# Score matmuls of differential attention heads issued for one head or for two at a time, with PSUM in three pools or in one

## The chip, the cores and the metric

The kernel runs on one core of a Trainium2 chip. The time is that of one execution on the device, in microseconds (us). The engines are TensorE (PE; its weight loads, which overlap its matmuls, are listed as PEld), VectorE (DVE), ScalarE (ACT), GpSimd (POOL) and SyncE (SP). Each works through its own stream of instructions in order; semaphores tie the streams together. PSUM, where matmuls put their results, has eight banks.

## What is computed

Two layers of an encoder with 256 tokens and a width of 2048, all in f32. The part that the change touches is differential attention: eight heads, two softmax maps each, over keys of 64 features.

```python
def diff_attention(q, k, v, lam):
    b, s = q.shape[:2]
    qh = q.reshape(b, s, DIFF_HEADS, 2, DIFF_HEAD_DIM)
    kh = k.reshape(b, s, DIFF_HEADS, 2, DIFF_HEAD_DIM)
    scale = DIFF_HEAD_DIM ** -0.5
    ...
        scores = jnp.einsum('bqhcd,bkhcd->bhcqk', qb, kh).astype(jnp.float32) * scale
        probs = jax.nn.softmax(scores, axis=-1)
        weights = probs[:, :, 0] - lam * probs[:, :, 1]
        return jnp.einsum('bhqk,bkhe->bqhe', weights.astype(v.dtype), v)
```

Around it, in each layer: one wide projection of the normalised input (queries, keys and values of this attention, the latents of a second one, two gates), multi-head latent attention with eight heads (MLA), the two outputs weighed by the gates and projected, a SwiGLU feed-forward part, and a gated addition of a projected side input. A final norm ends it.

## The kernel before

**Products.** Nearly all the time goes into products of a weight matrix and activations. Activations lie with features on the partitions, 128 features by 256 tokens to a tile, 16 tiles for the width. To keep precision, each f32 operand is split into two parts of a faster format: a high part, and the remainder. A tile of activations (`ua`, `ub`) holds both, high in its left half and the remainder in its right. A *chunk* of a product (`emit`, L226 and L230) is two matmuls: the high weights against both halves (512 columns), and the weights' remainder against the high half (256 columns). A product of the full width has 16 chunks. Weights come by DMA, up to eight chunks to a piece (`piece`), into one of four buffers; ACT makes the high part `whi` (L201) and DVE the remainder `wlo` (L78), each in three buffers. `joined` adds the two halves of a finished PSUM bank: ACT copies one half to SBUF, DVE adds the other.

**The stage around the change.** `values` makes the values of the differential heads. `queries_keys(h)` makes the query and the key of head h, two full products, with a partial rotation and a split on DVE and ACT; heads 0 and 1 are made first. `scores` (L428) then multiplies query by key, with 64 features (half of the array's rows) for each of the two maps. A map is three products of parts (`three`), for two blocks of 128 queries: six matmuls, twelve for a head. The maps lie on the lower and the upper 64 partitions, and the matmuls alternate between them. `exps` takes the maximum of every row on DVE (L434) and the exponentials on ACT (L437). `diff_weights(h)` joins both maps to one matrix of weights, ACT and DVE sharing that work. `diff_out` first transposes the weights on TensorE (`turned`, L446), and in a second part multiplies them with the values (L701).

**Order.** A scheduler orders each engine's stream when the program is built, by the order in which instructions are traced and by when its own model of time has them ready; `keep_in_program_order` pins an instruction behind the one traced before it on its engine, `issue_after` behind a named one. `beside` is a generator of other work to fill in, in 16 steps: queries and keys of heads 2 to 7, the MLA keys (`keys_up`), its rotary key (`narrow`, `rotated`), then gate products, MLA queries (`queries_up`) and the norm of finished heads (`settle`). `pipelined` traces, for each head: one fill step, the weights of the *next* head, the transposes of this one, one fill step, the output of this one. The MLA heads go through the same `pipelined` with `mla_weights`, which also uses `scores`, and gate products as fill.

**PSUM.** Three pools share the eight banks: `ps_mm`, four, for products; `ps_s`, two, for scores; `ps_at`, two, for transposes, outputs and norms. The end of the kernel, where the last two products are cut into halves and the result is transposed and stored, takes banks of all three.

Of the kernel before, what the change touches and what calls it, by code (L numbers as in the profile page):

```python
# [12 lines left out]
F32 = mybir.dt.float32  # L13
# [3 lines left out]
ALU = mybir.AluOpType  # L17
AX = mybir.AxisListType

P = 128  # L20
# [36 lines left out]
def encoder(ctx, tc, x, p, positions, cols, lams, wq, wk, wv, wcq, wckv, wkr, wga, wgb,  # L57
# [6 lines left out]
    wts = pool("wts")  # L64
    tmp = pool("tmp")
    stat = pool("stat")
    ps_mm = pool("ps_mm", 4, space=PSUM)
    ps_s = pool("ps_s", 2, space=PSUM)
    ps_at = pool("ps_at", 2, space=PSUM)

    def scratch(tag, bufs, n=T):
        return tmp.tile([P, n], F32, tag=tag, name=tag, bufs=bufs)

    def bank(ps=ps_at, tag="at", name="at", shape=(P, 2 * T)):
        return ps.tile(list(shape), F32, tag=tag, name=name)

    def tt(o, a, b, op):
        return V.tensor_tensor(out=o, in0=a, in1=b, op=op)  # L78
# [155 lines left out]
    def product(src, us, inside=None):  # L234


        acc = bank(ps_mm, "mm", "mm")
        n = len(us)
        for a in range(0, n, PT):
            m = min(PT, n - a)  # L240
            hi, lo = piece(src[:, a * P : (a + m) * P], m)
            emit(acc, hi, lo, 0, us[a : a + m], a == 0, a + m == n, inside and (inside[0] - a, inside[1]))
        return acc

    def pair(src, us):

        n = len(us)
        hi, lo = piece(src.rearrange("n p m -> p n m"), 2 * n)
        for j in range(2):
            acc = bank(ps_mm, "mm", "mm")  # L250
            emit(acc, hi, lo, j * n, us, True, True)
            yield acc

# [146 lines left out]
    def narrow(src, us):  # L400


        acc = bank(ps_mm, "mm", "mm")
        w = wts.tile([P, PT * P], F32, tag="w32", name="w32", bufs=W_BUFS)
        nc.sync.dma_start(w, src)
        w = w.rearrange("p (c m) -> p c m", m=64)
        for a in range(0, NC, PT):
            both = wts.tile([P, PT * P + 64], F32R, tag="whi", name="whi", bufs=3)[:, : PT * P]
            hi, lo = (both.rearrange("p (c f m) -> p c f m", f=2, m=64)[:, :, f, :] for f in range(2))
            part = w[:, a : a + PT, :]  # L410
            A.activation(hi, part, AF.Copy)
            tt(lo, part, hi.bitcast(F32), ALU.subtract)
            for j in range(PT):
                PE.matmul(acc, both[:, j * P : (j + 1) * P], us[a + j], start=a + j == 0, stop=a + j == NC - 1)  # L414
        return acc
# [1 line left out]
    def three(q, k):  # L417
        return [(q[:, :T], k[:, T:]), (q[:, T:], k[:, :T]), (q[:, :T], k[:, :T])]

    def scores(*maps):  # L420


        Ss = [bank(ps_s, "S", "S", (P, 2, T)) for _ in maps]
        for b in range(2):
            for j in range(len(maps[0])):
                for S, pairs in reversed(list(zip(Ss, maps))):
                    q, k = pairs[j]
                    PE.matmul(S[:, b, :], q[:, b * P : (b + 1) * P], k, start=j == 0, stop=j == len(pairs) - 1)  # L428
        return Ss

    def exps(S, E, scale):

        nm, sm, rs = (stat.tile([P, 2], F32, tag=t, name=t, bufs=4) for t in ("nm", "sm", "rsum"))
        V.tensor_reduce(out=nm, in_=S, axis=AX.X, op=ALU.max, negate=True)  # L434
        ts(nm, nm, scale, None, ALU.mult)
        for b in range(2):
            last_exp[0] = A.activation(E[:, b, :], S[:, b, :], AF.Exp, bias=nm[:, b : b + 1], scale=scale, accum_out=sm[:, b : b + 1])  # L437
        V.reciprocal(out=rs, in_=sm)
        return rs
# [20 lines left out]
    def weights(tag="E", dt=F32):  # L460
        return tmp.tile([P, 2, T], dt, tag=tag, name=tag, bufs=2)
# [12 lines left out]
    def values(src, us, load=None):  # L474

        vals = stat.tile([P, 2, 2, 512], F32, tag="vals", name="vals", bufs=1)
        n = len(us)
        order = [(half, a, 2) for half in range(2) for a in range(0, n, 2)]
        if load:
            order = [(None, a, 1) for a in range(BOTH)] + [(half, BOTH, n - BOTH) for half in range(2)]  # L480
        banks = {}
        for half, a, m in order:
            if a == 0:
                for k in (0, 1) if half is None else (half,):
                    banks[k] = [bank(ps_mm, "mm", "mmv") for _ in range(2)]
            if load and not half:
                load(a, m)
            if half is None:
                hi, lo = piece([src[k][:, a * 512 : (a + 1) * 512] for k in range(2)], 8, 32, 16)
            else:  # L490
                hi, lo = piece(src[half][:, a * 512 : (a + m) * 512], 4 * m, 32, 16)
            for j in range(2 if half is None else m):
                k, c = (j, a) if half is None else (half, a + j)
                s = slice(j * 512, (j + 1) * 512)
                if load and c == 0:
                    first_chunk(banks[k], us[0], hi[:, s], lo[:, s])
                    continue
                for b in range(2):
                    xh = us[c][:, b * P : (b + 1) * P]
                    xl = us[c][:, T + b * P : T + (b + 1) * P]  # L500
                    PE.matmul(banks[k][b], xh, hi[:, s], start=c == 0, stop=False)  # L501
                    PE.matmul(banks[k][b], xl, hi[:, s], start=False, stop=False)  # L502
                    last_mm[:] = [PE.matmul(banks[k][b], xh, lo[:, s], start=False, stop=c == n - 1)]  # L503
            if half or a + m < n:
                yield
            if a + m == n:
                for b in range(2):
                    A.activation(vals[:, b, half, :], banks[half][b], AF.Copy)
                if not half:
                    yield vals  # L510
# [16 lines left out]
    for L in range(DEPTH):  # L527
# [153 lines left out]
        od, ods = [], ub[:8]  # L681
        ssd = stat.tile([P, 2 * DH], F32, tag="ssd", name="ssd", bufs=1)

        def diff_weights(h):
            q, k = qk[h]
            E = [weights(), weights("E1")]
            halves = [slice(c * 64, (c + 1) * 64) for c in range(2)]
            r = [exps(S, e, 0.125) for S, e in zip(scores(*(three(q[d], k[d]) for d in halves)), E)]
            ts(r[1], r[1], neg_lam[:, L : L + 1], None, ALU.mult)
            for b in range(2):  # L690
                A.activation(E[0][:, b, :], E[0][:, b, :], AF.Copy, scale=r[0][:, b : b + 1])
                stt(E[0][:, b, :], E[1][:, b, :], r[1][:, b : b + 1], E[0][:, b, :], ALU.mult, ALU.add)
            return E[0]

        def diff_out(h, W):
            wt = turned(W)
# [30 lines left out]
                next(out, None)  # L727
                W = nxt

        pipelined(diff_weights, diff_out, DH, lambda: next(fill, None))  # L730
        for _ in fill:
            pass
        vm, = (v for v in values(w_v[L], ckv) if v is not None)
# [3 lines left out]
        def mla_weights(h):  # L737
            E = weights()
            t = slice(h % 2 * T, (h % 2 + 1) * T)
            S, = scores(three(qn[h], kn[h]) + [(qr[h // 2][:, t], krs[1][:, t]), (qr[h // 2][:, t], krs[0][:, :T])])  # L740
            r = exps(S, E, MLA_SCALE)
            for b in range(2):
                ts(E[:, b, :], E[:, b, :], r[:, b : b + 1], None, ALU.mult)
            return E
# [104 lines left out]

    for n in ends:  # L850
        parts[n] = [piece(w_pg[L, n][:, a * P : (a + PT) * P], PT) for a in (0, PT)]
        m = banks[n, 0] = bank(ps_mm, "mm", "mm")
        for j, u in enumerate(ub):
            w, (hi, lo) = slice(j % PT * P, (j % PT + 1) * P), parts[n][j // PT]
            if j < whole[n]:
                matmul(m, hi[:, w], u, start=j == 0, stop=False)
            else:
                matmul(halves_of(m)[:, :, :P], hi[:, w], halves_of(u)[:, :, :P], start=False, stop=False)
            matmul(m[:, T:], lo[:, w], u[:, :T], start=False, stop=j == NC - 1)
    for n in ends:  # L860
        m = banks[n, 1] = bank(ps_mm, "mm", "mm")
        for j in range(whole[n], NC):
            w = slice(j % PT * P, (j % PT + 1) * P)
            matmul(halves_of(m[:, :T]), parts[n][j // PT][0][:, w], halves_of(ub[j])[:, :, P:], start=j == whole[n], stop=j == NC - 1)
        tiles_[n] = [scratch(tag, bufs) for tag, bufs in (("join", 3), ("a", 4), ("sig", 2))]
# [55 lines left out]
    def store(b, q, o):  # L921
        tc.keep_in_program_order(nc.sync.dma_start(out[b, :, q * 2 * T : (q + 2) * 2 * T], o))

    def S_bank():
        return operand(bank(ps_s, "S", "S", (P, 2, T)))

    def mm_bank():
        return bank(ps_mm, "mm", "mm")

    def steps(which, n):  # L930
        for _ in range(n):
            tc.keep_in_program_order(next(which))
# [6 lines left out]
    column = factors(0)  # L939
    for which, n in ((column, 2), (third, 1), (second, 2), (third, 2), (column, 2)):  # L940
        steps(which, n)
    t0 = [transposed(0, q, get()) for q, get in enumerate((S_bank, S_bank, mm_bank, mm_bank))]
    t1 = [transposed(1, 0, mm_bank())]
    column = factors(1)
    t1.append(transposed(1, 1, mm_bank()))
    t1.append(transposed(1, 2, bank()))
    parts_ = [rows() for _ in range(4)]
    left, right = slice(0, 2 * T), slice(2 * T, 4 * T)
# [3 lines left out]
    for j in range(2):  # L952
        tc.keep_in_program_order(scaled(parts_[j][:, right], t0[2 * j + 1], cols_[0], V))
        steps(column, 2)
        store(0, 2 * j, parts_[j])
    t1.append(transposed(1, 3, S_bank()))
    for j in range(2):
        tc.keep_in_program_order(scaled(parts_[2 + j][:, left], t1[2 * j], cols_[1], V))
        scaled(parts_[2 + j][:, right], t1[2 * j + 1], cols_[1], A)
# [89 lines left out]
```

## Time and profile before

| | |
|---|---|
| median of three runs | 2825.36 us (2825.22 to 2825.99) |
| the profiled execution | 2825.16 us |
| its span, first to last instruction | 2823.4 us |
| granted TensorE clock | 0.999 |
| DMA, mean over the span | 188 GB/s |

The profile is of one execution. Busy time of an engine is the union of its instructions. Matmuls are pipelined and overlap, so what a matmul costs TensorE is the distance from its start to the start of the next. The chain of waits follows the work that ended last back to its beginning. A row of the timeline has the start and the length in us, the engine, the line, the operation, what it writes and reads, and a count where like instructions in sequence are merged; in square brackets stands the idle time before it and what ended it. A group of a tile's or a line's instructions has the shortest, median and longest duration in ns, and the first and last start in us.

### The profile page before, as it was taken

How to read it: one execution, taken by the hardware profiler on the slowest of the kernel's cores; microseconds unless marked ns; L12 is line 12 of the kernel's file. 1: busy time of each engine (PE TensorE's matmuls, PEld its weight loads, DVE VectorE, ACT ScalarE, POOL GpSimd, SP SyncE). 2: the span in 40 equal slices, each digit the busy share in tenths (PEclk: the TensorE clock that was granted, in tenths of full speed). 3: DMA queues.
4: the chain of work that ended last, by engine and by line, in shares of the span. 5: the costliest groups of instructions: out<-in, count | busy, mean ns of one | idle time of the engine just before them, and what ended most of it. 6: DMA issues, size and time to landing. Idle time of an engine off the chain costs nothing.

```text
span 2823.4 us, 43989 instructions
## 1 busy us (share of the span) xinstructions
PE 2815.7 (100%) x16691; PEld 2490.2 (88%) x16691; DVE 2078.9 (74%) x3566; ACT 1531.1 (54%) x2554; POOL 3.1 (0%) x17
## 2 busy tenths in 40 slices
PE   9999999999999999999999999999999999999999
PEld 8888988888888888888888889888888888888888
DVE  8898668776666666677869976687766666666777
ACT  7676546554444444455646765465544444444556
POOL 0000000000000000000000000000000000000000
PEclk9999999999999999999999999999999999999999
DMA  7544455555665565565554454555556655655664
GB/s 247 175 161 172 157 186 198 194 193 194 187 200 193 188 194 198 194 193 193 194 193 166 157 172 158 194 198 194 193 194 189 199 194 184 203 193 194 193 193 157
DMA packets 158181, 531.36 MB, mean 188 GB/s; under 512 B 17169, under 2 KB 25361, under 8 KB 157969
## 3 DMA queue, kind: packets, MB, share of 16 engines
q1 hardware_dynamic: 157536, 527.96, 57.0%
q8 instruction: 131, 2.15, 0.3%
q10 hardware_dynamic: 432, 0.59, 0.1%
q14 instruction: 82, 0.66, 0.1%
HBM read 526.39 MB, written 2.10 MB: 187 GB/s over the span
## 4 chain that ended last, share of the span: by engine, by line
PE 100%; DMA 0%; DVE 0%; DVEq 0%; ACT 0%; SPq 0%; issue 0%
PE mm L226 61%; PE mm L230 31%; PE S L428 1%; PE mmv L502 1%; PE mmv L503 1%; PE mmv L501 1%; PE at L446 1%; PE at L701 1%; PE mm L848 0%; PE at L757 0%; PE mm L414 0%; PE at L716 0%; PE mmv L472 0%; DMA w<-in_wv 0%; PE at L339 0%; PE at L307 0%
## 5 line engine op out<-in xcount | busy, mean ns | idle before, releaser
L201 ACT ACTIVATE whi<-w 128x1024 fp32r<-128x1024 f32 (+2 forms) x1038 | 1064.3, 1026 | 1226.8 <-issue 593.3
L78 DVE TENSOR_TENSOR wlo<-w,whi 128x1024 fp32r<-128x1024 f32 (+2 forms) x1038 | 1224.9, 1181 | 647.8 <-ACT whi L201 638.7
L226 PE MATMUL mm<-ub,whi 128*128 128x512 f32 x3936 | 1340.5, 389 | 0.0
L226 PE MATMUL mm<-ua,whi 128*128 128x512 f32 x3712 | 1274.2, 390 | 0.0
L230 PE MATMUL mm<-ub,wlo 128*128 128x256 f32 x3936 | 1084.6, 276 | 0.0
L230 PE MATMUL mm<-ua,wlo 128*128 128x256 f32 x3712 | 1027.7, 277 | 0.0
L226 PEld LDWEIGHTS mm<-ub,whi 128*128 128x128 f32 x3936 | 737.8, 188 | 151.5
L226 PEld LDWEIGHTS mm<-ua,whi 128*128 128x128 f32 x3712 | 696.3, 188 | 141.2
L230 PEld LDWEIGHTS mm<-ub,wlo 128*128 128x128 f32 x3936 | 738.9, 188 | 1.3
L230 PEld LDWEIGHTS mm<-ua,wlo 128*128 128x128 f32 x3712 | 697.0, 188 | 2.0
L78 DVE TENSOR_TENSOR a<-mm,join 128x256 f32<-128x256 f32 (+1 forms) x423 | 174.5, 416 | 1.7 <-ACT join L877 1.4
L256 ACT ACTIVATE join<-mm 128x256 f32<-128x256 f32 x452 | 165.2, 367 | 6.4 <-PE mm L230 5.7
L78 DVE TENSOR_TENSOR xT<-xT,mm 128x256 f32<-128x256 f32 x256 | 106.8, 420 | 41.6 <-PE mm L230 37.7
L78 DVE TENSOR_TENSOR a<-a,row 128x256 f32<-128x256 f32 (+1 forms) x209 | 87.5, 422 | 5.9
L78 DVE TENSOR_TENSOR a<-a 128x256 f32<-128x256 f32 x120 | 50.9, 425 | 4.0
L78 DVE TENSOR_TENSOR ua<-a,ua 128x256 fp32r<-128x256 f32 x120 | 49.9, 417 | 1.0 <-ACT ua L264 1.0
L264 ACT ACTIVATE ua<-a 128x256 fp32r<-128x256 f32 x120 | 48.2, 403 | 2.6 <-DVE a L78 2.6
L437 ACT ACTIVATE E<-S,nm 128x256 f32<-128x256 f32 x96 | 44.1, 471 | 8.2 <-DVE nm L84 8.2
L501 PE MATMUL mmv<-whi,ua 128*128 128x512 f32 x124 | 47.0, 391 | 0.0
L502 PE MATMUL mmv<-whi,ua 128*128 128x512 f32 x124 | 47.0, 392 | 0.0
L503 PE MATMUL mmv<-wlo,ua 128*128 128x512 f32 x124 | 41.2, 391 | 0.0
L78 DVE TENSOR_TENSOR ssq<-ssq,sq 128x256 f32<-128x256 f32 x96 | 40.1, 418 | 0.3 <-ACT sq L294 0.3
(214 smaller groups left out, 1211.5 us busy)
## 6 DMA issues: line engine op xcount, KB each, us to landing
w<-in_w_gate SPq DMA_DIRECT2D x176, 512.0 KB, 4.6
w<-in_w_up SPq DMA_DIRECT2D x176, 512.0 KB, 4.6
w<-in_w_down SPq DMA_DIRECT2D x128, 512.0 KB, 4.2
w<-in_wga SPq DMA_DIRECT2D x64, 512.0 KB, 3.7
w<-in_wgb SPq DMA_DIRECT2D x64, 512.0 KB, 3.8
w<-in_w_out SPq DMA_DIRECT2D x64, 512.0 KB, 4.6
w<-in_w_pg SPq DMA_DIRECT2D x64, 512.0 KB, 4.6
w<-in_w_down SPq DMA_DIRECT2D x64, 384.0 KB, 3.7
```

The source lines that it names most:

```text
L78: return V.tensor_tensor(out=o, in0=a, in1=b, op=op)
L201: last_split[:] = A.activation(hi[:, s], w[:, s], AF.Copy), tt(lo[:, s], w[:, s], hi[:, s].bitcast(F32), ALU.subtract)
L226: lead = PE.matmul(acc, hi[:, s], u, start=start, stop=False)
L230: rest = PE.matmul(acc[:, T:], lo[:, s], u[:, :T], start=False, stop=stop)
L256: A.activation(t, acc[:, T:], AF.Copy)
L264: return A.activation(hi, src, AF.Copy), tt(lo, src, hi.bitcast(F32), ALU.subtract)
L428: PE.matmul(S[:, b, :], q[:, b * P : (b + 1) * P], k, start=j == 0, stop=j == len(pairs) - 1)
L437: last_exp[0] = A.activation(E[:, b, :], S[:, b, :], AF.Exp, bias=nm[:, b : b + 1], scale=scale, accum_out=sm[:, b : b + 1])
L446: PE.transpose(tp[:, kb, b * P : (b + 1) * P], W[:, b, kb * P : (kb + 1) * P], ident)
L501: PE.matmul(banks[k][b], xh, hi[:, s], start=c == 0, stop=False)
L502: PE.matmul(banks[k][b], xl, hi[:, s], start=False, stop=False)
L503: last_mm[:] = [PE.matmul(banks[k][b], xh, lo[:, s], start=False, stop=c == n - 1)]
```

## The change

`diff_weights` takes two heads: their four maps go into one call of `scores`, which issues head h0 + 1's twelve matmuls and then head h0's, each pinned behind the instruction traced before it on TensorE. `scores` now takes a list of heads; for a single one (MLA) nothing is pinned. The differential heads leave `pipelined` for a loop of their own, which places the fill steps: two before the first pair's scores; behind the scores of each pair two (one for the last pair), then both heads' transposes, one step, both outputs, and one more step (none for the last pair). The sixteen steps are used up by it. All PSUM tiles come from one pool with one tag of eight banks, and the end of the kernel takes its banks there too.

```diff
-    ps_mm = pool("ps_mm", 4, space=PSUM)
-    ps_s = pool("ps_s", 2, space=PSUM)
-    ps_at = pool("ps_at", 2, space=PSUM)
+    ps = pool("ps", 8, space=PSUM)
...
-    def bank(ps=ps_at, tag="at", name="at", shape=(P, 2 * T)):
-        return ps.tile(list(shape), F32, tag=tag, name=name)
+    def bank(name="at", shape=(P, 2 * T)):
+        return ps.tile(list(shape), F32, tag="bank", name=name)
...
-    def scores(*maps):
+    def scores(*heads):
...
-        Ss = [bank(ps_s, "S", "S", (P, 2, T)) for _ in maps]
-        for b in range(2):
-            for j in range(len(maps[0])):
-                for S, pairs in reversed(list(zip(Ss, maps))):
-                    q, k = pairs[j]
-                    PE.matmul(S[:, b, :], q[:, b * P : (b + 1) * P], k, start=j == 0, stop=j == len(pairs) - 1)
+        Ss = [[bank("S", (P, 2, T)) for _ in maps] for maps in heads]
+        for banks, maps in zip(Ss, heads):
+            for b in range(2):
+                for j in range(len(maps[0])):
+                    for S, pairs in reversed(list(zip(banks, maps))):
+                        q, k = pairs[j]
+                        m = PE.matmul(S[:, b, :], q[:, b * P : (b + 1) * P], k, start=j == 0, stop=j == len(pairs) - 1)
+                        if len(heads) > 1:
+                            tc.keep_in_program_order(m)
         return Ss
...
-        def diff_weights(h):
-            q, k = qk[h]
-            E = [weights(), weights("E1")]
+        def diff_weights(h0):
             halves = [slice(c * 64, (c + 1) * 64) for c in range(2)]
-            r = [exps(S, e, 0.125) for S, e in zip(scores(*(three(q[d], k[d]) for d in halves)), E)]
-            ts(r[1], r[1], neg_lam[:, L : L + 1], None, ALU.mult)
-            for b in range(2):
-                A.activation(E[0][:, b, :], E[0][:, b, :], AF.Copy, scale=r[0][:, b : b + 1])
-                stt(E[0][:, b, :], E[1][:, b, :], r[1][:, b : b + 1], E[0][:, b, :], ALU.mult, ALU.add)
-            return E[0]
+            pairs = [[three(qk[h][0][d], qk[h][1][d]) for d in halves] for h in (h0 + 1, h0)]
+            Ws = []
+            for Ss in scores(*pairs):
+                E = [weights(), weights("E1")]
+                r = [exps(S, e, 0.125) for S, e in zip(Ss, E)]
+                ts(r[1], r[1], neg_lam[:, L : L + 1], None, ALU.mult)
+                for b in range(2):
+                    A.activation(E[0][:, b, :], E[0][:, b, :], AF.Copy, scale=r[0][:, b : b + 1])
+                    stt(E[0][:, b, :], E[1][:, b, :], r[1][:, b : b + 1], E[0][:, b, :], ALU.mult, ALU.add)
+                Ws.append(E[0])
+            return Ws[::-1]
...
-        pipelined(diff_weights, diff_out, DH, lambda: next(fill, None))
+        def steps_on(n):
+            for _ in range(n):
+                next(fill)
+
+        steps_on(2)
+        for h in range(0, DH, 2):
+            last = h + 2 == DH
+            Ws = diff_weights(h)
+            steps_on(1 if last else 2)
+            outs = [diff_out(h + j, Ws[j]) for j in range(2)]
+            for part in outs:
+                next(part)
+            steps_on(1)
+            for part in outs:
+                next(part, None)
+            if not last:
+                steps_on(1)
         for _ in fill:
             pass
...
-    t0 = [transposed(0, q, get()) for q, get in enumerate((S_bank, S_bank, mm_bank, mm_bank))]
-    t1 = [transposed(1, 0, mm_bank())]
+    t0 = [transposed(0, q, get()) for q, get in enumerate((bank, bank, bank, bank))]
+    t1 = [transposed(1, 0, bank())]
     column = factors(1)
-    t1.append(transposed(1, 1, mm_bank()))
+    t1.append(transposed(1, 1, bank()))
     t1.append(transposed(1, 2, bank()))
...
-    t1.append(transposed(1, 3, S_bank()))
+    t1.append(transposed(1, 3, bank()))
```

More of the change, by code (lines that the diff above doesn't have):

```diff
@@ L234, in product @@
     def product(src, us, inside=None):
-        acc = bank(ps_mm, "mm", "mm")
+        acc = bank("mm")
         n = len(us)
@@ L249, in pair @@
         for j in range(2):
-            acc = bank(ps_mm, "mm", "mm")
+            acc = bank("mm")
             emit(acc, hi, lo, j * n, us, True, True)
@@ L400, in narrow @@
     def narrow(src, us):
-        acc = bank(ps_mm, "mm", "mm")
+        acc = bank("mm")
         w = wts.tile([P, PT * P], F32, tag="w32", name="w32", bufs=W_BUFS)
@@ L484, in values @@
                 for k in (0, 1) if half is None else (half,):
-                    banks[k] = [bank(ps_mm, "mm", "mmv") for _ in range(2)]
+                    banks[k] = [bank("mmv") for _ in range(2)]
             if load and not half:
@@ L739, in mla_weights @@
             t = slice(h % 2 * T, (h % 2 + 1) * T)
-            S, = scores(three(qn[h], kn[h]) + [(qr[h // 2][:, t], krs[1][:, t]), (qr[h // 2][:, t], krs[0][:, :T])])
+            (S,), = scores([three(qn[h], kn[h]) + [(qr[h // 2][:, t], krs[1][:, t]), (qr[h // 2][:, t], krs[0][:, :T])]])
             r = exps(S, E, MLA_SCALE)
@@ L851, in encoder @@
         parts[n] = [piece(w_pg[L, n][:, a * P : (a + PT) * P], PT) for a in (0, PT)]
-        m = banks[n, 0] = bank(ps_mm, "mm", "mm")
+        m = banks[n, 0] = bank("mm")
         for j, u in enumerate(ub):
@@ L860, in encoder @@
     for n in ends:
-        m = banks[n, 1] = bank(ps_mm, "mm", "mm")
+        m = banks[n, 1] = bank("mm")
         for j in range(whole[n], NC):
@@ L922, in store @@
         tc.keep_in_program_order(nc.sync.dma_start(out[b, :, q * 2 * T : (q + 2) * 2 * T], o))
[L924 to L928, printed above, removed]
     def steps(which, n):
```

## The prediction

> **What bounds the kernel now.** I read the page's first and fourth parts, then TensorE's waits, and then, because TensorE turned out never to wait, its instructions by start time around the scores.
>
> ```profile
> PE 2815.7 (100%) x16691; PEld 2490.2 (88%) x16691; DVE 2078.9 (74%) x3566; ACT 1531.1 (54%) x2554; POOL 3.1 (0%) x17
> PE 100%; DMA 0%; DVE 0%; DVEq 0%; ACT 0%; SPq 0%; issue 0%
> PE at L517 <- DVE ones L123: 1.1, 1, 1.1
> PE mmv L472 <- ACT whi L201: 0.3, 1, 0.3
> L428 PE MATMUL S<-fa,ub x192: 273/277/385, 106.4 to 1610.4; 64*128 64x256 f32 x192
> ```
>
> The first line is the page's table of engines, the second the chain that ended last: TensorE (PE) is busy throughout and the chain is its own instruction stream. The next two are all its waits in the trace, 1.4 us, both in the first microseconds, before any attention. So no wait remains that a change in the middle could remove; time can leave only if TensorE's own stream gets shorter, and can come in only if a new wait appears on it. The last row is the object of the change: 192 score matmuls of the differential heads, on 64 rows of the array. Twelve belong to a head, so there are 16 runs of twelve, eight in each layer.
>
> Busy time says nothing about what such a run costs, since matmuls overlap (277 ns each, by the row, but far closer together). What counts is the distance from start to start. The timeline of TensorE around the first run:
>
> ```profile
> 106.18 0.28 PE L230 MATMUL mm<-ub,wlo 128*128 128x256 f32 x1
> 106.38 0.97 PE L428 MATMUL S<-fa,ub 64*128 64x256 f32 x12
> 107.29 0.50 PE L226 MATMUL mm<-ub,whi 128*128 128x512 f32 x1
> 107.62 0.28 PE L230 MATMUL mm<-ub,wlo 128*128 128x256 f32 x1
> ...
> 107.98 0.28 PE L230 MATMUL mm<-ub,wlo 128*128 128x256 f32 x1
> 108.09 0.39 PE L226 MATMUL mm<-ub,whi 128*128 128x512 f32 x1
> 108.32 0.28 PE L230 MATMUL mm<-ub,wlo 128*128 128x256 f32 x1
> ```
>
> ```profile
> 106.73 0.63 PE L428 MATMUL S<-fa,ub 64*128 64x256 f32 x8
> 106.96 0.40 PE L428 MATMUL S<-fa,ub 64*128 64x256 f32 x4
> ```
>
> The columns are start, length, engine, line, operation and count. Undisturbed, L230 holds the stream for 0.11 us (107.98 to 108.09) and L226 for 0.23 (108.09 to 108.32), 0.34 for one chunk of a product. The two rows of the second fence are the same run, cut by two narrower windows: its last eight matmuls begin at 106.73, its last four at 106.96. They go two by two, one on each half of the array, so two pairs take 0.23, **0.115 us a pair**; six pairs are worth 0.69.
>
> **What a run costs beyond its work.** The L230 at 106.18 should have passed after 0.11, and took 0.20: 0.09 lost going in. The run lasts 0.91 (106.38 to 107.29): 0.22 more than six pairs; the first four matmuls alone take 0.35 (to 106.73) in place of 0.23. The L226 behind it takes 0.33 in place of 0.23: 0.10. Together **0.41 us** where a product follows. What is late is the weights:
>
> ```profile
> 106.38 0.77 PEld L428 LDWEIGHTS S<-fa,ub 64*128 64x128 f32 x12 [0.24 <-issue]
> 107.29 0.19 PEld L226 LDWEIGHTS mm<-ub,whi 128*128 128x128 f32 x1
> ```
>
> The first score weights and the first weights behind the run start together with their matmuls (106.38, 107.29), and the score loads stood idle for 0.24 before. At each change between half and whole array the weights aren't loaded ahead. Where transposes follow:
>
> ```profile
> 123.50 0.39 PE L226 MATMUL mm<-ua,whi 128*128 128x512 f32 x1
> 123.82 0.98 PE L428 MATMUL S<-fa,ub 64*128 64x256 f32 x12
> 124.73 0.66 PE L446 MATMUL at<-ident,E 128*128 128x128 f32 x4
> 125.14 0.36 PE L230 MATMUL mm<-ua,wlo 128*128 128x256 f32 x1
> ```
>
> ```profile
> 189.12 0.60 PE L446 MATMUL at<-ident,E 128*128 128x128 f32 x4
> 189.48 0.36 PE L230 MATMUL mm<-ua,wlo 128*128 128x256 f32 x1
> ```
>
> ```profile
> 123.89 0.91 PE S L428 x12
> 124.80 0.59 PE at L446 x4
> ...
> 174.94 0.90 PE S L428 x12
> 175.85 0.59 PE at L446 x4
> ```
>
> In: 0.32 against 0.23, 0.09. The run again 0.91 from start to start, 0.22 over. Four transposes take 0.41 behind scores, 0.36 at 189.12 with none ahead: 0.05. Together **0.36 us**. The last four rows are the chain of waits: first and last of the five runs of layer one that transposes follow; the other three meet products. Layer two repeats this. So the 16 runs carry 10 x 0.36 + 6 x 0.41 = **6.06 us** that is no work.
>
> **The change part by part.**
>
> *Scores in pairs.* 192 matmuls stay 192, with the same operands; 16 runs become 8 of 24. The score matmuls are pinned behind the product traced before them, and the pair's transposes are traced two steps later, so I take it that products follow every run: 8 x 0.41 = 3.28. Saved: 6.06 - 3.28 = **2.78 us**. If transposes followed all of them it would be 6.06 - 2.88 = 3.18; if the step from one head to the other inside the 24 cost as much as a run's start, 8 x 0.22 = 1.76 would come back and 1.0 be left. No run of 24 is in this trace; nearest are the pairs inside a run, which pass from one accumulation to the next at 0.115, so I take nothing for that step.
>
> The Trainium skill, TensorEngine Tiling (Array Packing), Key Properties, says that changing the tiling mode, "not just tile", drains the array. By it the step between heads, which keeps the mode, is free and the saving 2.78; by a rule that charged any new operand set it would be 1.0. The trace agrees inside a run (0.115 a pair) and cannot show the head step.
>
> *Order of the fill work.* The same 16 steps are taken, in another grouping: two ahead of the first scores, then two, one and one around each pair; nothing is added to SP's or POOL's queue, and the weight DMAs keep their order. The pin adds a possible wait: whatever TensorE has left would stand behind a score run whose keys are late. But the last key of every pair is traced at least one step ahead, mostly a product pair of 2 x 16 x 0.34 = 10.9 us, so I take 0. Transposes and output matmuls of two heads stand together; the rows price no gain for that, and I take 0, between 0 and 0.4 (0.05 for each of eight joints). It also moves what runs before which product, and that has a price:
>
> ```profile
> 86.95 0.40 PE L226 MATMUL mm<-ua,whi 128*128 128x512 f32 x1
> ...
> 87.30 0.40 PE L226 MATMUL mm<-ua,whi 128*128 128x512 f32 x1
> ```
>
> Here a chunk takes 0.35 (86.95 to 87.30), not 0.34. Over one product of 16 chunks that is 0.16. If each of eight new groups gains or loses such a product, 1.3 us either way: I take 0 and keep both ends. The edit moves no SBUF tile, as it touches PSUM pools alone.
>
> *Softmax in pairs.* DVE and ACT do the same instructions, four maps in one lot. Behind DVE's waiting maximum stand the weight remainders that TensorE's next products need.
>
> ```profile
> 100.00:115.00 15.00, 15.00 (x97) 13.15 (x96) 14.86 (x36) 11.19 (x25) 0.00 (x0) 1.00 0.39 133
> 115.00:130.00 15.00, 15.00 (x99) 13.12 (x98) 15.00 (x37) 11.16 (x27) 0.00 (x0) 1.00 0.64 217
> ```
>
> ```profile
> 108.94 1.28 DVE L434 TENSOR_REDUCE nm<-S 128x2 f32<-128x512 f32 x2
> ...
> 112.15 0.16 DVE L84 TENSOR_SCALAR nm<-nm 128x2 f32<-128x2 f32 x1
> 112.21 1.22 DVE L78 TENSOR_TENSOR wlo<-w,whi 128x1024 fp32r<-128x1024 f32 x1
> ```
>
> ```profile
> L81 DVE SCALAR_TENSOR_TENSOR E<-E,rsum,E x32: 465/478/486, 120.3 to 1620.2; 128x256 f32<-128x256 f32 x32
> 114.10 0.28 PE L230 MATMUL mm<-ua,wlo 128*128 128x256 f32 x1
> ```
>
> The first fence has two windows of 15 us (sum, then PE, PEld, DVE, ACT with their counts): DVE is full, 14.86 and 15.00. The second is DVE's timeline, the last rows the group of weighted sums and a moment of TensorE's timeline. A head costs it two maxima, 1.28, two weighted sums, 0.96, and five small ones of about 0.16: 3.0, so a pair about 6. The reserve at its lowest: matching remainders and products in order, the one ready at 113.43 (112.21 + 1.22) is first used at 114.10, 0.67 us later. Latent norm and the first softmax press on DVE together there (the window's 14.86), and still TensorE did not wait. The change parts those two, as its first scores come after two steps of products; and a lot of 6 us stands against a reserve of up to three split pieces, 3 x 8 x 0.34 = 8.2 us. I take 0. If that cover is gone, each pair costs what the lot exceeds the reserve by, at most 6 us.
>
> *One ring of eight banks.* It adds no instruction. Four banks now hold scores at once where two did, with four left for products, transposes and outputs. A bank's cost as a wait isn't shown, as TensorE has none; from below it is nothing, and as there is no bank wait to remove, no gain. From above, a product kept from a bank until a head's maxima are read, 1.28 us, once for each pair: 10.2. I take 0, nearest to the rows of waits. The tail's banks change names only: its transposes never wait now.
>
> **Sum.** The profiled execution took 2825.16 us, its span 2823.4 and 1.8 around it; it is 0.2 under the median of the runs shown, 2825.36. 2825.16 - 2.78 = 2822.4, about 0.1% off.
>
> **Rivals.**
>
> *Starved by DVE (slower).* The pair's 6 us delays the remainders, and TensorE waits in products behind each run. For it: windows at 99 and 100%, a reserve that fell to 0.67. Against: the heavier crowd at 105 to 112 was borne. The measurement of this kernel can tell about 0.2%, 5.65 us, from no change; this turns to slower once a pair costs (5.65 + 2.78) / 8 = 1.05 us. At 1.25 it is 2822.4 + 10 = **2832**. Chance 0.12, of which a little stays under the bound.
>
> The Trainium skill, TensorEngine Tiling (Array Packing), PSUM Bottleneck, warns that tiling speeds up TensorE but not the emptying of PSUM, which may then bind. That is this rival; four maxima of 0.64 per run are its price here, and no wait in this trace shows it yet.
>
> *The runs don't hold.* If one of four banks comes late, the scheduler lets a product in between the heads, and 16 runs remain: **2825**. For it: four banks asked for at once. Against: eight in all, and the instructions are chained. Chance 0.14.
>
> *More than the runs.* The slow stretches go too and the joints gain their 0.4, and transposes follow: 2825.16 - 3.2 - 1.3 - 0.4 = **2820.3**; every such end at its best still stays near 0.2%. Chance 0.08.
>
> **How the numbers follow.** The forecast, 2822.4, gets 0.66: with 1.3 for stretches either way and 1.0 to 3.2 for the runs it reaches from 2820.7 to 2825.5. For eight in ten I add the broken runs and small waits of up to 0.5 us a pair, 2826.5, and leave out the starved case and half of the last. Faster by over 0.2% needs a gain that no row offers: 0.03. Slower: most of the starved case and a little for the ring, 0.11. The rest, 0.86, is the same.
>
> **What would show it.** Right: eight rows of 24 score matmuls on the chain, each about 1.6 us (12 x 0.115 plus 0.22), followed by products; TensorE's waits still 1.4 us. Wrong: runs split in twelves; a wait of TensorE on a remainder, a split or a bank in 105 to 220; chunks at 0.35 in more places. The forecast falls if a pair's softmax shows up as idle TensorE, or if the step between heads inside a run costs another 0.2.

## The result and the profile after

| | before | after |
|---|---|---|
| median, same comparison | 2825.49 us (4 runs) | 2875.91 us (4 runs, 2873.61 to 2877.66) |
| ratio | | 1.0178, 95% interval 1.0166 to 1.0191 |
| the profiled execution | 2825.16 us | 2873.61 us |
| its span | 2823.4 us | 2871.8 us |
| granted TensorE clock | 0.999 | 0.995 |

The kernel became 1.8% slower, 50 us, where 2.8 us less was forecast and 2826.5 was the end of the range. TensorE's waits in the trace of after (us in total, times, longest):

```profile
PE at L720 <- DVE fa L82: 14.6, 2, 7.3
PE at L447 <- DVE E L79: 8.0, 4, 3.7
PE at L378 <- DVE a L76: 7.7, 2, 3.9
PE at L705 <- ACT wt L452: 3.3, 3, 1.5
PE mm L224 <- ACT whi L199: 1.1, 1, 1.1
PE at L518 <- DVE ones L121: 1.1, 1, 1.1
PE S L427 <- DVE fa L76: 0.8, 2, 0.4
PE mm L228 <- DVE wlo L76: 0.8, 1, 0.8
```

TensorE waited 1.4 us before and waits 37.4 now (the sum of the rows): 36.0 of the 48.4 us by which the span grew. Nearly all of it, 33.6, stands in the first four rows, and these aren't products and aren't scores. They are small things that come between products: transposes of a norm's result (L720), of attention weights (L447), of the rotary key (L378), and output matmuls (L705). Each waits for a softmax, a norm or a rotation on DVE and ACT, as it had to before. What is new is that TensorE does nothing else meanwhile.

The score runs themselves, in TensorE's timeline of after around the second pair:

```profile
150.11 0.28 PE L228 MATMUL mm<-ua,wlo 128*128 128x256 f32 x1
150.31 1.68 PE L427 MATMUL S<-fa,ub 64*128 64x256 f32 x24
151.92 0.53 PE L224 MATMUL mm<-ub,whi 128*128 128x512 f32 x1
152.28 0.29 PE L228 MATMUL mm<-ub,wlo 128*128 128x256 f32 x1
```

0.09 us lost going in (150.11 to 150.31, where 0.11 is due), 1.61 for 24 (twelve pairs at 0.115 are 1.38, so 0.23 over), and 0.13 behind (151.92 to 152.28, where 0.23 is due): 0.45 beyond the work, once for two heads. There are eight such rows and no run is broken.

So the saving is there and 36 us of waits beside it. That would make 2825.2 - 2.8 + 36.0 = 2858.4; 15 us more are missing. Most of them lie behind the waits. Here is TensorE's timeline of after around the longest one (its first row is the last four of 16 output matmuls), and the windows of the same stretch (sum, then PE, PEld, DVE, ACT, POOL with their counts, the granted clock, DMA share, GB/s):

```profile
248.70 0.61 PE L705 MATMUL at<-vals,wt 128*128 128x128 f32 x4
256.63 1.73 PE L720 MATMUL at<-ident,fa 128*128 128x128 f32 x7 [7.32 <-DVE fa L82]
...
258.79 0.63 PE L224 MATMUL mm<-ua,whi 128*128 128x512 f32 x1
...
259.43 0.63 PE L224 MATMUL mm<-ua,whi 128*128 128x512 f32 x1
...
262.63 0.27 PE L720 MATMUL at<-ident,fa 128*128 128x128 f32 x1
```

```profile
249.30:256.60 7.30, 0.01 (x1) 0.01 (x1) 6.91 (x28) 2.75 (x11) 0.00 (x0) 0.86 0.28 97
256.60:261.50 4.90, 4.87 (x18) 4.24 (x19) 2.57 (x10) 1.33 (x3) 0.00 (x0) 0.51 0.01 3
261.50:266.00 4.50, 4.50 (x28) 3.91 (x27) 1.62 (x2) 2.04 (x3) 0.00 (x0) 1.00 0.02 7
```

After 7.3 us of standing still TensorE has half its clock: 0.51 in the second window. A chunk takes 0.64 us there (258.79 to 259.43) in place of 0.34, and only the third window has the full clock again. Such a wait is thus paid twice, once while it lasts and once in slow work behind it.

### The profile page after: what moved, and what is told of

The parts are those of the page before. It is cut to its first block, busy times and chain, and to the rows that moved or that the text cites. A ratio compares the mean times of both kernels' runs of the same rounds, so it can differ in the third digit from the quotient of the medians.

```text
span 2871.8 us, 43933 instructions
## 1 busy us (share of the span) xinstructions
PE 2828.1 (98%) x16691; PEld 2498.9 (87%) x16691; DVE 2084.7 (73%) x3566; ACT 1533.7 (53%) x2554; POOL 3.1 (0%) x17
## 4 chain that ended last, share of the span: by engine, by line
PE 95%; DVE 2%; ACT 2%; issue 1%; DMA 0%; SPq 0%; DVEq 0%; ACTq 0%
PE mm L224 59%; PE mm L228 30%; PE mmv L503 1%; PE mmv L504 1%; PE mmv L502 1%; ACT E L438 1%; PE S L427 1%; ACT whi L199 1%; DVE wlo L76 1%; DVE nm L435 1%; PE at L447 0%; PE at L705 0%; PE mm L868 0%; PE at L777 0%; DVE a L76 0%
## 5 line engine op out<-in xcount | busy, mean ns | idle before, releaser
L438 ACT ACTIVATE E<-S,nm 128x256 f32<-128x256 f32 x96 | 44.6, 478 | 13.6 <-DVE nm L82 13.4
```

## Where the longest wait comes from

The transposes at L720 belong to `settle`, the norm of finished heads. Its first and last steps on DVE, in the timeline of after, and then in that of before:

```profile
251.06 0.17 DVE L82 TENSOR_SCALAR rv<-ssd 128x8 f32<-128x8 f32 x1
...
256.19 1.66 DVE L82 TENSOR_SCALAR fa<-fa,ry 128x128 f32<-128x128 f32 x8
```

```profile
237.17 0.17 DVE L84 TENSOR_SCALAR rv<-ssd 128x8 f32<-128x8 f32 x1
...
246.58 1.66 DVE L84 TENSOR_SCALAR fa<-fa,ry 128x128 f32<-128x128 f32 x8
```

Before, DVE took even longer over this norm (from 237.17 to 248.24, against 251.06 to 257.85). TensorE's timeline of before shows why that cost nothing:

```profile
242.91 0.39 PE L428 MATMUL S<-fb,fa 128*128 128x256 f32 x2
...
250.20 0.38 PE L716 MATMUL at<-ident,fa 128*128 128x128 f32 x2
...
255.24 0.38 PE L716 MATMUL at<-ident,fa 128*128 128x128 f32 x2
255.38 0.48 PE L226 MATMUL mm<-ua,whi 128*128 128x512 f32 x1
...
256.17 0.39 PE L226 MATMUL mm<-ua,whi 128*128 128x512 f32 x1
256.40 0.38 PE L716 MATMUL at<-ident,fa 128*128 128x128 f32 x2
```

The transposes (L716 there) come two at a time from 250.20 to 256.40, the first some 3 us after their data, the last 8 us after all of them were ready (248.24), between the chunks of products. Scores of the first MLA head, which are traced after the whole of `settle`, have passed them at 242.91. In the kernel after, TensorE's stream has 16 output matmuls and then at once seven transposes of the norm: the products traced behind them stay behind them. Only the eighth transpose, which shares its bank with the seventh, comes later, at 262.63, between products.

From this came two theories. **R**, for ring: a bank is handed out in the order of tracing, and with one ring of eight for everything, an instruction that wants a bank can't be placed ahead of one that was traced earlier and has none yet. A product then cannot pass a transpose that waits, and TensorE follows the order in which the code first asks for each bank. With separate pools the two kinds of work have separate queues for banks. **D**, for DVE, is the prediction's starved case: four softmax maps in one lot press on DVE and ACT, and TensorE waits for what they owe it. A third, **P**, is that the pin behind the scores holds the stream.

## The experiments

**The ring alone.** The kernel before, with its three pools made one and nothing else changed:

```diff
-    ps_mm = pool("ps_mm", 4, space=PSUM)
-    ps_s = pool("ps_s", 2, space=PSUM)
-    ps_at = pool("ps_at", 2, space=PSUM)
+    ps = pool("ps", 8, space=PSUM)
```

> The kernel before with its three PSUM pools made one pool of eight banks, and nothing else changed: heads one at a time, 16 runs of 12. Theory R (one pool hands out banks in the order in which tiles are traced, so that TensorE's products can no longer run ahead of a transpose that waits for DVE): TensorE shows waits at the transposes and outputs, and the time is well over the changed kernel's loss, 2850 to 2930 us, as each head's transposes are traced straight behind the next head's scores. Theory D (the doubled softmax lot starves TensorE through DVE): no pairs here, so no loss, 2825 us and waits of 1.4 us.

Measured: 2938.18 us, ratio 1.040 (1.0386 to 1.0414), a little beyond R's upper end and far from D's; span 2935.3, granted clock 0.982. TensorE's waits, the first three rows:

```profile
PE S L426 <- DVE fa L76: 51.9, 10, 9.8
PE at L714 <- DVE fa L82: 16.4, 2, 8.2
PE S L426 <- DVE ra L76: 9.5, 2, 4.8
```

Without any pairing the ring costs 113 us, more than twice the whole change. The scores wait most, for their own query or key (`fa`), which DVE is still rotating. In the kernel before, products are placed ahead of them until that is done. So D alone can't be the cause, and under a ring the other half of the change is even a help: it traces scores a step or two behind their keys, and the row of scores that wait for `fa`, 51.9 us here, has 0.8 in the kernel after.

**Pairs, with the products' banks apart.** The kernel after, with four banks for products and four for the rest:

```diff
-    ps = pool("ps", 8, space=PSUM)
+    ps = pool("ps", 4, space=PSUM)
+    ps_mm = pool("ps_mm", 4, space=PSUM)
...
+        if name[:2] == "mm":
+            return ps_mm.tile(list(shape), F32, tag="mm", name=name)
```

> The changed kernel, with four banks kept for products and one pool of four for scores, transposes, outputs and norms. Theory R: products run ahead again, TensorE's waits fall from 37 us to a few, the eight runs of 24 stay, and the time is 2822.4 us, 2.8 under the kernel before. Theory D: the pairs are still there, and with them the waits: about 2870 us.

Measured: 2826.84 us (11 runs), ratio 1.0007 (0.9998 to 1.0016), span 2824.6. With one line of pools changed, 49 of the 50 us are gone, and the pairs with all their softmax lots are still there. That is R, and it clears D of the bulk. But it is 4 us above what R gave. The waits of TensorE in this run, and ACT's and DVE's timelines where they fall:

```profile
PE mm L231 <- DVE wlo L79: 1.5, 2, 0.8
...
PE mm L227 <- ACT whi L202: 0.6, 2, 0.3
```

```profile
128.37 1.28 ACT L441 ACT_TABLE_LOAD   x1
...
133.13 0.51 ACT L441 ACTIVATE E<-S,nm 128x256 f32<-128x256 f32 x1
...
133.58 1.09 ACT L202 ACTIVATE whi<-w 128x1024 fp32r<-128x1024 f32 x1
```

```profile
134.71 1.22 DVE L79 TENSOR_TENSOR wlo<-w,whi 128x1024 fp32r<-128x1024 f32 x1 [0.52 <-ACT whi L202]
```

Here is D, in small: the split of the next weights stands on ACT behind a load of the exponential's table and all eight exponentials of the first pair, and TensorE waits for it and then for the remainder. Start to start it loses 1.5 us in each layer, at the first pair and at no other. Two such losses, against the 2.8 that the runs should save (2.5 at 0.45 us a run), would put it 0.2 to 0.5 us above before. The median is 1.8 above (2826.84 beside 2825.06 in the same comparison), though the interval of the ratio still holds 1, and where the rest comes from isn't shown.

**The control for that split.** The kernel before, heads one by one, with the banks of scores and transposes put together and the products' left apart:

```diff
-    ps_s = pool("ps_s", 2, space=PSUM)
-    ps_at = pool("ps_at", 2, space=PSUM)
+    ps_at = ps_s = pool("ps", 4, space=PSUM)
```

> The kernel before with its scores' and its other two banks made one pool of four, products keeping their own four: the pools of e2 without the pairs. Theory R: the scores and transposes are handed their banks in traced order, but products are free, so at most a few us of waits: 2825 to 2835 us. The distance to e2 is then what pairs alone are worth. Theory D: 2825 us.

Measured: 2825.92 us, ratio 1.0003 (0.9994 to 1.0011). Two pools in place of three cost nothing that shows. The four corners, then, medians in us:

| | products' banks apart | one ring of eight |
|---|---|---|
| heads one by one | 2825.9 | 2938.2 |
| heads in pairs | 2826.8 | 2875.9 |

**The ring, with two products traced ahead.** If the order in which the code asks for banks has become TensorE's order, then moving lines should move the wait. Two gate products go from behind `settle(4)` to in front of it:

```diff
+            for _ in range(2):
+                gate(wga, gate_a, next(todo))
             settle(4)
             for n in (4, 6):
-                gate(wga, gate_a, next(todo))
                 queries_up(n)
```

> The changed kernel, in which the fill work traces two gate products ahead of the second norm's transposes in place of behind them; the same instructions in all. Theory R: order of tracing is order of issue, so the two waits of 7.3 us at these transposes go, with the slow products behind them: 2876 to about 2858 us, and the other waits stay. Theory D: the order of tracing changes nothing in DVE's load, the waits move elsewhere: 2876 us.

Measured: 2857.58 us, ratio 1.0116 (1.0102 to 1.0129). The row of L720, 14.6 us, is gone, and the other transposes' rows stay:

```profile
PE at L447 <- DVE E L79: 8.9, 6, 3.7
PE at L378 <- DVE a L76: 7.7, 2, 3.8
```

By the medians it takes 18.3 us less, as R has it. The two profiled executions differ by less: 14.2 us of span (2871.8 and 2857.6) for 13.6 us of waiting (37.4 and 23.8, all rows), at the same granted clock of 0.995. So the wait went with the lines that were moved; what the slow work behind it was worth, this pair doesn't show.

**The ring without the pin.** From `scores` only this is taken:

```diff
-                        if len(heads) > 1:
-                            tc.keep_in_program_order(m)
```

> The kernel after the change with the pin taken from the scores, so that the scheduler may place the 24 score matmuls freely; the ring of eight stays. R (one ring hands its banks out in traced order, so nothing of TensorE passes an instruction that is traced earlier): nothing changes, 2873 to 2879 us, TensorE's waits again about 37 us and on the same rows (at on fa, at on E, at on a). P (the pin holds TensorE's stream back): the waits go and it takes about 2825 us.

Measured: 2873.17 us, ratio 1.0169 (1.0154 to 1.0185), and the waits on the same rows, `at` on `fa` again 14.6. P falls. What the pin does is keep the runs whole: without it the second pair's run breaks in 2 and 22 in both layers.

**Transposes apart, products with the scores.** Two banks for transposes, outputs and norms, and a ring of six:

```diff
-    ps = pool("ps", 8, space=PSUM)
+    ps = pool("ps", 2, space=PSUM)
+    ps_mm = pool("ps_mm", 6, space=PSUM)
...
+        if name != "at":
+            return ps_mm.tile(list(shape), F32, tag="mm", name=name)
```

> The kernel after the change with its eight banks in two pools: two for transposes, outputs and norms, six for scores and products. R: what cost the time was products kept in line behind transposes that wait for a softmax or a norm; with the two apart products may pass them, TensorE's waits fall from 37 to under 5 us, and it takes 2824 to 2828 us. If scores and products in one ring were the costly pair (the products kept behind a maximum that is still to be read), it stays above 2850.

Measured: 2839.27 us, ratio 1.0051 (1.0039 to 1.0064): between the two expectations. The waits of transposes are gone, as R has it, but TensorE now waits 9.8 us in products, in four places. DVE's and TensorE's timelines at the first:

```profile
123.75 0.68 DVE L438 TENSOR_REDUCE nm<-S 128x2 f32<-128x512 f32 x1
...
124.49 0.41 DVE L79 TENSOR_TENSOR a<-mm,join 128x256 f32<-128x256 f32 x1
```

```profile
121.81 0.28 PE L231 MATMUL mm<-ub,wlo 128*128 128x256 f32 x1
124.95 0.79 PE L227 MATMUL mm<-ua,whi 128*128 128x512 f32 x1 [2.87 <-DVE a L79]
125.55 0.41 PE L231 MATMUL mm<-ua,wlo 128*128 128x256 f32 x1
...
126.19 0.41 PE L231 MATMUL mm<-ua,wlo 128*128 128x256 f32 x1
```

With four of six banks under scores, products have two. The next product begins when DVE has emptied one (`a<-mm`, done at 124.90), and that stands behind maxima. By these rows it is a true wait for a bank, the one the prediction had bounded, and it is a different thing from the order that cost the 50 us.

**Cover for the first pair.** In the kernel with pairs and products apart, a gate product is moved to right behind the first pair's scores:

```diff
             Ws = diff_weights(h)
+            if h == 0:
+                gate(wga, gate_a, next(todo))
```

> e2 (pairs, products in four banks of their own) with one gate product of each layer moved from the end of the fill work to right behind the first pair's scores, where in e2 the split weights came late by 1.6 us in each layer. If that was the first pair's softmax standing ahead of the splits (S, a small form of D), a product of 5.4 us covers it: 3.2 us go and it takes 2823.6 us, the saving of the eight runs, faster than the kernel before by 0.06%. If what was late is the lot of splits itself and no cover helps, the wait moves behind the moved product and it stays at 2826 to 2827.

Measured: 2830.56 us, ratio 1.0019 (1.0010 to 1.0028), above both expectations. The splits came late all the same and TensorE's waits in the middle rose from 2.1 us to 4.5, 2.5 on splits and 2.0 on remainders. More work for TensorE doesn't cover it. The likely reason, not tested apart, is that the added product needs splits of its own from the same ACT.

**A split ahead on ACT.** In the same kernel, four exponentials of the first pair are put behind one split of weights:

```diff
+            if h == 0:
+                for i in held:
+                    tc.add_manual_dep(i.ins, firsts[n].ins.name, NO_SYNC, reason="splits ahead")
```

> e2 (pairs, products in four banks of their own) with one split of weights put ahead of the second head's exponentials on ACT, in the first pair of each layer; in e2 it stood behind all eight exponentials, began at 133.6, and TensorE waited 1.5 us in each layer. If ACT's order there is what is left of the cost (A), these waits go and the saving of the eight runs shows: 2825.1 - 2.8 = 2822.3 to 2823.5 us, faster than the kernel before by 0.06 to 0.1%. If DVE's lot is what is left (D), the remainder is still late by about as much and it stays at 2826 to 2827.

Measured: 2828.85 us, ratio 1.0013 (1.0004 to 1.0022), again above both expectations. TensorE's waits on splits are gone and 1.2 us on remainders are left, but the rest of the stream was ordered anew, and in both layers the second pair's run broke. In TensorE's timeline:

```profile
149.86 0.97 PE L432 MATMUL S<-fa,ub 64*128 64x256 f32 x12
...
153.14 0.38 PE L432 MATMUL S<-fa,ub 64*128 64x256 f32 x1
...
153.88 0.98 PE L432 MATMUL S<-fa,ub 64*128 64x256 f32 x11
```

So it prices neither A nor D cleanly. The pin holds an instruction behind the one before it, but lets others in between.

**The first two heads one by one.** Products' banks apart, and only heads 2 to 7 of each layer in pairs:

```diff
-        steps_on(2)
-        for h in range(0, DH, 2):
+        W, = diff_weights(0)
+        steps_on(1)
+        nxt, = diff_weights(1)
+        for h, w in enumerate((W, nxt)):
...
+        for h in range(2, DH, 2):
```

> e2 (products in four banks of their own) with the first two heads of each layer weighed one by one, as before the change, and only the other six in pairs: 4 runs of 12 and 6 of 24 in place of 16 of 12. If e2's loss is all in the first pair, where latent norm, splits and softmax meet (A and D alike), no wait of the middle is left and 6 x 0.36 to 0.41 = 2.2 to 2.5 us of the runs' cost is saved: 2823 us, faster than the kernel before by 0.08%. If any pair costs as much as its run saves, it stays at 2825 to 2826.5.

Measured: 2823.84 us (11 runs) beside 2825.09 (15 runs), ratio 0.9995 (0.9986 to 1.0004); span 2821.4, 2.0 under that of before. One row of waits is left in the whole trace, that of the first microseconds:

```profile
PE at L521 <- DVE ones L124: 1.1, 1, 1.1
```

Only the first pair starved TensorE; three pairs in each layer add no wait. At the first pair the latents' norm, many splits and a change of ACT's table meet, and which of them it takes was not told apart. For six runs less the median falls by 1.25 us and the profiled span by 2.0, but the interval holds 1, so the run isn't shown to be faster.

**The price of a passage.** Two kernels made from the one before, heads one by one, each with 16 extra matmuls of a constant on the whole array, their results never read. In the first they stand in the middle of each run of twelve, in the second ahead of it:

```diff
+                if len(maps) == 2 and b == 1 and j == 0:
+                    extra = bank()
+                    m = PE.matmul(extra[:, :P], ones, ones, start=True, stop=True)
+                    tc.keep_in_program_order(m)
```

> The kernel before with one extra 128x128 matmul of a constant, on the whole array, in the middle of each of the 16 runs of twelve (after six score matmuls), pinned there; its result is never read. W (what a run costs beyond its work is paid once for each passage between half and whole array): 16 x (0.41 + 0.11) = 8.3 us more than before, about 2833.4, and the rows of twelve scores split in six and six. If a run's extra cost belongs to the run's first operands and not to the passage, only 16 x 0.11 = 1.8 us more, about 2827.

> The control of e8: the same 16 extra matmuls on the whole array, each traced just ahead of a run of twelve and not in its middle; the result is never read. W: 16 x 0.11 = 1.8 us more than before and no further passage, about 2827; together with e8 the price of a passage there and back is then (2835.0 - 2827) / 16 = 0.5 us. If an added matmul and its bank cost something by themselves, it comes near e8's 2835.

Measured: 2835.01 us (ratio 1.0034, 1.0022 to 1.0046) and 2829.82 (1.0016, 1.0007 to 1.0025). TensorE's timelines of the first run, the one and then the other:

```profile
107.24 0.62 PE L432 MATMUL S<-fa,ub 64*128 64x256 f32 x6
107.79 0.49 PE L428 MATMUL at<-ones 128*128 128x128 f32 x2
108.21 0.62 PE L432 MATMUL S<-fa,ub 64*128 64x256 f32 x6
108.76 0.50 PE L226 MATMUL mm<-ub,whi 128*128 128x512 f32 x1
```

```profile
106.84 0.38 PE L428 MATMUL at<-ones 128*128 128x128 f32 x2
107.15 0.97 PE L432 MATMUL S<-fa,ub 64*128 64x256 f32 x12
108.06 0.50 PE L226 MATMUL mm<-ub,whi 128*128 128x512 f32 x1
```

The extra matmul is two instructions, not the one that the expectation reckoned with, so the control is 4.3 us above before and not 1.8. Between the two kernels only the place differs: 1.52 us (107.24 to 108.76) against 1.22 (106.84 to 108.06), 0.30 for one passage there and back. By the spans it is (2833.6 - 2828.3) / 16 = 0.33. The price belongs to the passage between half and whole array and is paid each time, as W has it, at 0.3 where no product follows.

## Why the prediction was wrong, step by step

**What bounds the kernel: right.** TensorE alone, no wait left to remove; time could come in only as a new wait on it. That is how it came: 36 us of waits and the slow clock behind them.

**Scores in pairs: right, in mechanism and size.** Forecast were eight runs at 0.41 us beyond their work; they take 0.45, and the step from head to head is free. The rule of draining the array (the Trainium skill, TensorEngine Tiling (Array Packing), Key Properties) agrees with 1.61 us for the run of 24, and with the passage of 0.30 us that the two kernels with extra matmuls priced. What it is worth is the other matter: six runs fewer moved the span by 2.0 us and the median by 1.25, where 2.2 to 2.5 were reckoned.

**One ring of eight banks: the step that failed.** The prediction wrote "It adds no instruction" and took 0, "nearest to the rows of waits". Its upper end, 10.2 us, asked only whether there were banks enough. The pools had a second work, which no row of waits could show, since it kept waits from arising: they let products pass transposes, outputs and scores that weren't ready. The ring alone takes that away and costs 113 us; in the kernel after it is 49 (2875.9 against 2826.8). The rows that would have told it stood in the trace of before: the norm's scaling on DVE at 246.58 and its transposes on TensorE from 250.20 to 256.40, between the chunks of products and behind scores traced later. The prediction read the waits and the runs, and never asked why there were no waits.

That R is the cause rests on the pools (four corners), on the moved products and on the kernel without the pin. How the scheduler comes to this order stays open; that banks are given out in traced order is the reading that fits all of these.

The Trainium skill, Perfetto Trace Analysis, Matmul Optimizations, says to see that all eight PSUM banks are used, for the most parallelism between instructions. Both kernels use all eight. How they are divided decided here: heads one by one or in pairs, one pool for all was the slowest of the divisions tried.

**Order of the fill work: right where it spoke of the pin**, which costs nothing that shows (2873.2 without it); the 0.4 us for which the first pair of each layer waits for `fa` is there without it too. It missed that under a ring the order in which banks are asked for becomes the order of TensorE.

**Softmax in pairs: mechanism real, mis-sized, and not what decided.** Taken as 0; in the kernel with products apart it is 1.5 us for the first pair of each layer and none for the others, 3 us against the 2.8 that the runs save. The starved rival asked for it in each of eight pairs, 10 us, by DVE. It was two pairs, and ACT's queue, on which the prediction put no price, came first. This eats what the runs save, so that even the good division of banks shows no gain.

**The rivals.** None of the named ones had the ring as a mechanism. Of the 0.11 for slower "a little" was for the ring, as a want of banks and not as an order. The 0.12 for the starved case had the sign right and the wrong cause; "the runs don't hold" fell in the change, all eight being whole, but broken runs do occur, in the kernels without the pin and with a split ahead.

## What to carry to other kernels

Where a bound engine never waits, ask what keeps it from waiting before touching buffers: look for work in its stream that comes long after its data were ready, between pieces traced later, and see which pools let it. Under this scheduler, pools of PSUM are also lanes for order; keep long, always-ready products in one of their own, apart from short work that hangs on a softmax or a norm. A change that bundles a small gain with a change of pools should be priced as two.

## What the runs showed of the hardware

Half a clock after a pause was not expected. In the kernel after, the granted clock is 0.51 in the 4.9 us behind a wait of 7.3. In the kernel with transposes apart, 2.87 us of waiting already do it: the granted clock is 0.50 from 124.95 to 127.00, and the chunk at 125.55 takes 0.64 us (to 126.19). The views of mean clock, after and the ring alone:

```profile
core 0: 2871.8 us, clock 0.995
```

```profile
core 0: 2935.3 us, clock 0.982
```

By these, 0.004 and 0.017 of the span more than before are short of the full clock, 11 and 50 us, an estimate with steps of 3; these are upper ends for what it costs, since part of the slow clock falls into the waits themselves (0.86 in the first of the three windows above). In the ring alone the waits grew by 80.4 us, which leaves 31.5 of the 111.9 by which the span grew. In the kernel after, 2871.8 - 2823.4 - 36.0 + 2.8 = 15.2 us lie beyond the waits. Counting the half clock only where TensorE works, over the whole traces, gives 11 us there and 32 in the ring alone. In the ring alone that is all of the rest, and in the kernel after the larger part; some 4 us of it stay open.

The Trainium skill, TensorE: Matmul & The Clock Gate, Part 1: The HAM clock gate, has the array's clock at half its rate after an idle window of about 3.4 us, the windows running freely, until a busy one has passed. The 0.51 and the doubled chunk agree with the two rates. The wait of 2.87 us is shorter than that window and was followed by half the clock all the same, so here a pause needn't reach 3.4 us to cost twice.
